# An encoder kernel in fp32r: finishes spread over the scan stage's iterations, and partial sums kept in the matmul banks of the last stages

## The chip, the cores and the metric

The kernel runs on one core of one Trainium2 chip. The time is device microseconds of one launch, and the median over runs is compared. The engines are TensorE (PE in the profile, with its weight loads PEld), VectorE (DVE), ScalarE (ACT), GpSimd (POOL) and SyncE (SP), whose queue issues the DMAs.

## What is computed

One layer of an encoder trunk over a prompt of 1024 tokens and a sample of 512, with 1024 channels. The parts that matter here:

```python
h = _rmsnorm(x, norm_g)
proj = jnp.einsum('bld,de->ble', h, w_in)
(q, f_fw, f_bw, i, z_a, c_B, c_C, c_x, z_b, g_a, g_b) = jnp.split(proj, SPLIT_POINTS, axis=-1)
o_a = _hgrn2_bidir(q, i, f_fw, f_bw, lb_fw, lb_bw, hnorm_g).astype(x.dtype)
p_a = jnp.einsum('ble,ed->bld', o_a * jax.nn.silu(z_a), w_a)
conv = _centred_short_conv(c_C * c_x, conv_w, conv_b)
p_b = jnp.einsum('ble,ed->bld', c_B * conv * jax.nn.silu(z_b), w_b)
merged = jax.nn.sigmoid(g_a) * p_a + jax.nn.sigmoid(g_b) * p_b
return x + jnp.einsum('bld,de->ble', merged, w_o)
```

`_hgrn2_bidir` is a gated linear recurrence in both directions, 8 heads of 128 channels, and a norm per head. A last norm over the channels ends the trunk.

## The kernel before

Every float32 matmul is done as three passes over split operands (`hi`, `lo`; PASSES): ScalarE makes `hi` (L63, "w_h", "s_h"), VectorE the rest (L64, "w_l", "s_l"). Large products of the prompt go by Strassen's scheme in Winograd's form: seven products for eight, with sums of operands before and sums of results after.

Up to 884 us norms and projections run, untouched by the change. Then comes the **scan stage**, to about 1520. Its loop (L670 to L707) has three iterations for each head: the two blocks of the head's prompt group and its sample, m = 0, 1, 2. In an iteration the block loaded before (`prev`) gets its near scores, its keys transposed (L500, copied by ScalarE as kT, L502), its scores (L451, L485) and its contributions (L513: key times value, copied by ScalarE to us, L514); the current block gets its decays (L437, L438 on VectorE, with copies "cat" L435, L436 on ScalarE). Between them stand units: projections of the sample (pp L77), of 24 matmuls each. `outputs` (L537) fills the one bank "o", ScalarE squares and scales it into oz (L541, L545), with a root by GpSimd (rs_o). `finish` (L547 to L553) transposes oz back into a bank "u" (L551), VectorE multiplies it with a gate zg (L552), and it is stored. Banks "u" are three, shared by key transposes, contributions and finishes. In this stage the order on TensorE is the order in which the code is written (order_pe, closed at L989); on the other engines a scheduler sets it, and each engine works its queue in order.

Before the change both blocks of the prompt and the sample's block are finished in iteration m = 2: the prompt's behind the first unit, the sample's ahead of the contributions.

The **last stages** follow from 1591 on: w_b for the prompt, w_b for the sample (from 1667), w_a for the prompt (from 1711), w_a for the sample (from 1787), and the output (from 1830). A prompt stage takes pairs of rows of blocks: `Rows` loads two raws, makes sums S on VectorE (L795 to L800) and splits of 128x1024 (w_h, w_l); `two_blocks` (L820 to L856) then does seven products of 12 matmuls each (L829), every one in a bank "pw" of its own, of five. ScalarE copies the first product, B11, to c11 (L838); VectorE adds T2, T3 and T1 to it in turn (`plus`, L833) and the result is used with an operand more (`use`). The operands of B21 and B22 (`last`, L844) are loaded and split during the first pair, behind its T2; so B21 comes late there. There are 14 pairs: four each in w_b and w_a, six in the output. Here the scheduler sets the order on all engines, TensorE too.

## Time and profile before

| | us |
|---|---|
| runs | 1966.63, 1958.93, 1961.59 (median 1961.59) |
| profiled execution | 1959.61 |
| its span in the trace | 1957.8 |
| TensorE busy | 1918.9 |
| VectorE busy | 1462.7 |
| ScalarE busy | 941.5 |
| mean granted clock of TensorE | 0.993 |

The profiled execution is 1.8 us longer than its span. Busy times are sums over the span; which engine sets the time of a stage is read from what ended each engine's idle time there. A row "PE u L513 <- DVE oz L552" says that TensorE's instruction of line 513, writing a tile u, stood idle until VectorE's instruction of line 552, writing oz, was done.

### The profile page before, as it was taken

Reading aid. Unit: us, or ns where it says so; the run is one execution under the profiler, and the core shown is the slowest. Engines: PE = TensorE matmul, PEld = TensorE weight load, DVE = VectorE, ACT = ScalarE, POOL = GpSimd, SP = SyncE. Lnnn points to the kernel's source line nnn. Section 1 sums busy time; section 2 is a strip of 40 time slices with the busy share of each in tenths; the row PEclk is TensorE's granted clock in tenths of the full one; section 3 lists DMA queues with packets and bytes.
Section 4 is the critical chain, followed back from the end, with each engine's and each line's share of the span. In section 5 each row is a group of like instructions: output and inputs, shape, how many; then the busy total and the mean of one; then the engine's idle time right before and its main releaser. Section 6 shows DMA issues by size and latency. Waiting matters only on the chain.

```text
span 1957.8 us, 38000 instructions
## 1 busy us (share of the span) xinstructions
PE 1918.9 (98%) x14772; PEld 1619.0 (83%) x14772; DVE 1462.7 (75%) x2423; ACT 941.5 (48%) x1946; POOL 144.4 (7%) x220
## 2 busy tenths in 40 slices
PE   8999999999999999999989999999999999999998
PEld 8988888888888888887878888888888888888786
DVE  6558787878787878785776577777773547889996
ACT  6433434434444343434676576676674333434432
POOL 1000000000000000002221122121220000000000
PEclk8999999999999999999999999999999999999999
DMA  7466676676676767668755554554534866879852
GB/s 211 125 212 233 231 232 235 228 238 226 227 245 217 241 230 242 230 211 318 254 184 193 205 196 167 203 198 162 207 132 172 321 232 208 278 236 303 295 175 76
DMA packets 306436, 427.35 MB, mean 218 GB/s; under 512 B 26192, under 2 KB 178000, under 8 KB 306256
## 3 DMA queue, kind: packets, MB, share of 16 engines
q1 hardware_dynamic: 306256, 424.93, 63.9%
q8 instruction: 116, 1.90, 0.4%
q14 instruction: 64, 0.52, 0.1%
HBM read 254.98 MB, written 169.87 MB: 217 GB/s over the span
## 4 chain that ended last, share of the span: by engine, by line
PE 79%; DVE 7%; DMA 4%; issue 4%; ACT 4%; POOL 1%; SPq 0%; DVEq 0%; POOLq 0%; ACTq 0%
PE pp L308 39%; PE pp L77 17%; PE pw L829 9%; PE pp L201 5%; PE pw L77 2%; DVE Q L438 2%; PE o L537 2%; PE u L513 2%; PE sc L451 1%; ACT cat L436 1%; DMA w_raw<-in_w_a 1%; PE pp L70 1%; DVE K L437 1%; POOL rs_o L81 1%; PE u L500 1%
## 5 line engine op out<-in xcount | busy, mean ns | idle before, releaser
L308 PE MATMUL pp<-s_h,w_h 128*128 128x512 f32 x1120 | 435.9, 389 | 1.2 <-ACT w_h L63 1.2
L308 PE MATMUL pp<-s_l,w_h 128*128 128x512 f32 x1120 | 435.7, 389 | 0.0
L308 PE MATMUL pp<-s_h,w_l 128*128 128x512 f32 x1120 | 435.7, 389 | 0.0
L77 PE MATMUL pp<-s_h,w_h 128*128 128x512 f32 x632 | 252.7, 400 | 1.4 <-DMA v<-v_d 0.8
L63 ACT ACTIVATE w_h<-w_raw 128x512 fp32r<-128x512 f32 (+1 forms) x204 | 141.2, 693 | 230.2 <-PE pp L308 151.8
L308 PEld LDWEIGHTS pp<-s_h,w_h 128*128 128x128 f32 x1120 | 210.2, 188 | 45.4 <-ACT w_h L63 1.9
L77 PE MATMUL pp<-s_h,w_l 128*128 128x512 f32 x632 | 247.4, 391 | 0.0
L77 PE MATMUL pp<-s_l,w_h 128*128 128x512 f32 x632 | 246.8, 391 | 0.0
L308 PEld LDWEIGHTS pp<-s_h,w_l 128*128 128x128 f32 x1120 | 210.2, 188 | 43.6
L308 PEld LDWEIGHTS pp<-s_l,w_h 128*128 128x128 f32 x1120 | 210.2, 188 | 43.6
L313 DVE TENSOR_TENSOR tmp<-pp,tmp 128x512 f32<-128x512 f32 x240 | 165.4, 689 | 104.1 <-PE pp L308 103.1
L63 ACT ACTIVATE w_h<-w_S 128x512 fp32r<-128x512 f32 x160 | 99.2, 628 | 186.8 <-PE pp L308 79.6
L64 DVE TENSOR_TENSOR w_l<-w_raw,w_h 128x512 fp32r<-128x512 f32 (+1 forms) x204 | 155.8, 765 | 37.4 <-ACT w_h L63 37.1
L829 PE MATMUL pw<-s_h,w_l 128*128 128x512 f32 x392 | 152.7, 390 | 2.0 <-DVE w_l L64 2.0
L829 PE MATMUL pw<-s_h,w_h 128*128 128x512 f32 x392 | 152.7, 390 | 1.6 <-ACT w_h L63 1.6
L829 PE MATMUL pw<-s_l,w_h 128*128 128x512 f32 x392 | 152.5, 389 | 0.0
L435 ACT COPY cat<-K 128x512 f32<-128x512 f32 x168 | 112.0, 670 | 61.1 <-DVE K L437 23.7
L77 PEld LDWEIGHTS pp<-s_h,w_l 128*128 128x128 f32 x632 | 119.0, 188 | 25.8
L77 PEld LDWEIGHTS pp<-s_h,w_h 128*128 128x128 f32 x632 | 119.5, 189 | 25.0 <-ACT K L132 1.1
L77 PEld LDWEIGHTS pp<-s_l,w_h 128*128 128x128 f32 x632 | 119.6, 189 | 23.4
L436 ACT COPY cat<-Q 128x512 f32<-128x512 f32 x168 | 112.4, 669 | 47.4 <-DVE Q L438 38.3
L438 DVE TENSOR_TENSOR Q<-Q,T 128x512 f32<-128x512 f32 x144 | 111.1, 772 | 27.1 <-ACT cat L436 25.3
(187 smaller groups left out, 3297.9 us busy)
## 6 DMA issues: line engine op xcount, KB each, us to landing
w_raw<-in_w_in SPq DMA_DIRECT2D x80, 512.0 KB, 5.3
ws_d<-w_h SPq DMA_DIRECT2D x160, 256.0 KB, 2.5
ws_d<-w_l SPq DMA_DIRECT2D x160, 256.0 KB, 2.5
w_h<-ws_d SPq DMA_DIRECT2D x79, 512.0 KB, 3.4
w_l<-ws_d SPq DMA_DIRECT2D x79, 512.0 KB, 5.4
fkq_d<-sg SPq DMA_DIRECT2D x48, 256.0 KB, 2.3
v_raw<-in_w_in SPq DMA_DIRECT2D x32, 256.0 KB, 3.5
fkq_d<-sk SPq DMA_DIRECT2D x32, 256.0 KB, 2.3
```

The source lines that it names most:

```text
L63: A.activation(hi, src, AF.Copy)
L64: V.tensor_tensor(lo, src, hi.bitcast(F32), op=ALU.subtract)
L77: T.matmul(out, whl[a][:, k, :], rhs(k, b), start=k == 0 and n == 0, stop=k == KT - 1 and n == 2)
L201: T.matmul(pp, B[f"B{k // 4 + 1}{t + 1}"][a][:, k % 4, c * P:(c + 1) * P], parts[k][b], start=k == 0 and m == 0, stop=k == KT - 1 and m == 2)
L308: T.matmul(bank, hl[x][:, k, :], B[b][y][:, k, :], start=k == 0 and i == 0, stop=k == 3 and i == 2)
L313: V.tensor_tensor(out, p, t, op=ALU.add)
L435: A.copy(ap(cat, 0, [[2 * hs, nb], [hs, 2], [1, hs]]), kall)
L436: A.copy(ap(cat, TB, [[2 * hs, nb], [hs, 2], [1, hs]]), qall)
L438: V.tensor_tensor(qall, qall, ap(t, 1, [[2, nb], [m - 1, 2], [0, hs]]), op=ALU.mult)
L513: T.matmul(p[:, c, :], kT[:, c, :], g.v[:, k.b * CPB + c, :], start=True, stop=True)
L537: T.matmul(p[:, c, :], l, r, start=m == 0, stop=m == len(mms) - 1)
L829: T.matmul(bank, hl[x][:, c:c + P], O[n][y][:, k, :], start=k == 0 and i == 0, stop=k == 3 and i == 2)
```

## The change

`finish` takes one block. Each iteration of the scan finishes one block right behind the key transposes: the sample of the head before last in m = 0, the prompt's two blocks in m = 1 and 2. The outputs of the prompt's second block and of the sample move ahead of the second unit of their iteration, behind the contributions. The gate zgp is loaded right behind the finish.

In the last stages `two_blocks` goes. B11 of a pair is begun while the pair before runs (`begun`); T2, T3 and T4 then add into the same bank, and ScalarE copies the bank between them (c11, u2, u3). B22 adds into T1's bank. VectorE adds a copy to a bank once in each use, and the adds `plus` are gone. `last()` comes directly behind the first product of a stage.

```diff
--- before.py
+++ after.py
@@ -544,8 +544,8 @@
                 for c in range(CPB):
                     A.activation(oz[:, c, :], p[:, c, :], AF.Copy, scale=r[:, c:c + 1])
 
-        def finish(g):
-            for k in g.done:
+        def finish(g, b):
+            for k in g.done[b:b + 1]:
                 p = bank("u", 3)
                 for c in range(CPB):
                     T.transpose(p[:, c, :], k.oz[:, c, :], ident)
@@ -677,29 +677,24 @@
             if prev:
                 near_scores(prev)
                 transpose_keys(prev)
+            if i > 3:
+                finish(*((sample[h - 2].g, 0) if m == 0 else (groups[h - 1], m - 1)))
             if m == 0 and h:
                 outputs(groups[h - 1], 0)
+            if m == 2:
+                groups[h].zg = gtile("zgp", [2 * TB])
+                load(groups[h].zg, zg_d[h])
             if cur:
                 decays(cur)
                 if cur.b == 0:
                     values(cur.g)
             unit()
-            if m == 2 and h:
-                finish(groups[h - 1])
             if prev:
                 scores(prev)
-            if m == 2:
-                if h:
-                    finish(sample[h - 1].g)
-                groups[h].zg = gtile("zgp", [2 * TB])
-                load(groups[h].zg, zg_d[h])
-            if prev:
                 contributions(prev)
+            if m < 2 and h:
+                outputs(*((sample[h - 1].g, 0) if m else (groups[h - 1], 1)))
             unit()
-            if m == 0 and h:
-                outputs(groups[h - 1], 1)
-            if m == 1 and h:
-                outputs(sample[h - 1].g, 0)
             if m != 1:
                 unit()
             if prev and len(prev.g.done) == len(prev.g.tbs):
@@ -707,8 +702,9 @@
             prev = cur
         outputs(sample[NH - 1].g, 0)
         unit()
-        finish(groups[NH - 1])
-        finish(sample[NH - 1].g)
+        for b in range(2):
+            finish(groups[NH - 1], b)
+        finish(sample[NH - 1].g, 0)
         left.close()
         right.close()
 
@@ -814,46 +810,56 @@
         def products(O, last, r, srcs, use):
 
 
-
+            def prod(hl, half, n, bank=None):
+                start = bank is None
+                if start:
+                    bank = ps.tile([P, TB], F32, name="pw", bufs=5)
+                for k in range(4):
+                    for i, (a, b) in enumerate(PASSES):
+                        c = half * TB + k * P
+                        T.matmul(bank, hl[a][:, c:c + P], O[n][b][:, k, :],
+                                 start=start and k == 0 and i == 0, stop=k == 3 and i == 2, skip_group_check=True)
+                return bank
+
+            def copied(bank):
+                c = wk.tile([P, TB], F32, name="c", bufs=6)
+                A.copy(c, bank)
+                return c
+
+            def begun(r):
+                r.x = prod(r.f, 0, "B11")
+                r.c11 = copied(r.x)
+
+            begun(r)
+            last()
             i = 0
             while r.raws:
-                r = two_blocks(O, r, partial(use, i), None if i else last, partial(srcs, i + 1))
+                if i:
+                    r.sums(0)
+                    r.sums(1)
+                ahead = Rows(srcs(i + 1))
+                if i == 0:
+                    y = prod(r.s12, 0, "T1")
+                prod(r.s12, 1, "T2", r.x)
+                u2 = copied(r.x)
+                if i == 0:
+                    ahead.first()
+                    begun(ahead)
+                else:
+                    y = prod(r.s12, 0, "T1")
+                prod(r.s34, 0, "T3", r.x)
+                u3 = copied(r.x)
+                use(i, 0, 0, prod(r.f, 1, "B21"), r.c11)
+                use(i, 1, 1, y, u3)
+                prod(r.last, 0, "T4", r.x)
+                use(i, 1, 0, r.x, None)
+                if i and ahead.raws:
+                    ahead.first()
+                    begun(ahead)
+                prod(r.s34, 1, "B22", y)
+                use(i, 0, 1, y, u2)
+                r = ahead
                 i += 1
-
-        def two_blocks(O, r, use, last, later):
-            def prod(hl, half, n):
-                bank = ps.tile([P, TB], F32, name="pw", bufs=5)
-                for k in range(4):
-                    for i, (x, y) in enumerate(PASSES):
-                        c = half * TB + k * P
-                        T.matmul(bank, hl[x][:, c:c + P], O[n][y][:, k, :], start=k == 0 and i == 0, stop=k == 3 and i == 2)
-                return bank
-
-            def plus(out, p, t):
-                V.tensor_tensor(out, p, t, op=ALU.add)
-
-            c11, c12, c21 = (wk.tile([P, TB], F32, name="c", bufs=6) for _ in range(3))
-            if not last:
-                r.first()
-            A.copy(c11, prod(r.f, 0, "B11"))
-            if not last:
-                use(0, 0, c11, prod(r.f, 1, "B21"))
-                r.sums(0)
-            plus(c12, prod(r.s12, 1, "T2"), c11)
-            if last:
-                last()
-            else:
-                r.sums(1)
-            ahead = Rows(later())
-            plus(c21, prod(r.s34, 0, "T3"), c12)
-            p5 = prod(r.s12, 0, "T1")
-            plus(c12, p5, c12)
-            use(1, 1, c21, p5)
-            use(1, 0, c21, prod(r.last, 0, "T4"))
-            if last:
-                use(0, 0, c11, prod(r.f, 1, "B21"))
-            use(0, 1, c12, prod(r.s34, 1, "B22"))
-            return ahead
 
         def plain(whl, act):
             pp = ps.tile([P, TB], F32, name="pw", bufs=5)
@@ -893,10 +899,11 @@
                         pb[j] = io.tile([P, 2, TB], F32, name="io")
                         load(pb[j].rearrange("p a b -> p (a b)"), pb_x[0][j])
 
-            def use(i, m, t, c, more):
+            def use(i, m, t, u, more):
                 m += 2 * i
-                u = wk.tile([P, TB], F32, name="sum", bufs=2)
-                V.tensor_tensor(u, more, c, op=ALU.add)
+                if more is not None:
+                    V.tensor_tensor(more, u, more, op=ALU.add)
+                    u = more
                 finish_block(m, t, s[m], u)
 
             r = prepared(srcs)
@@ -917,8 +924,8 @@
             pb = {}
 
             def block(m, t, s, u):
-                V.tensor_tensor(u, u, s[:, t, :], op=ALU.mult)
-                V.tensor_tensor(s[:, t, :], u, pb[m][:, t, :], op=ALU.add)
+                V.tensor_tensor(s[:, t, :], u, s[:, t, :], op=ALU.mult)
+                V.tensor_tensor(s[:, t, :], s[:, t, :], pb[m][:, t, :], op=ALU.add)
                 left_of[m] = left_of.get(m, 0) + 1
                 if left_of[m] == 2:
                     store(m_x[0][m], s.rearrange("p a b -> p (a b)"))
@@ -951,7 +958,8 @@
                 n = 2 * i + m
                 x = xt[n][:, h, :]
                 V.tensor_tensor(x, c, x, op=ALU.add)
-                V.tensor_tensor(x, more, x, op=ALU.add)
+                if more is not None:
+                    V.tensor_tensor(x, more, x, op=ALU.add)
                 A.activation(ps.tile([P, TB], F32, name="junk"), x, AF.Square, scale=D ** -0.5, accum_out=ss[n][:, h:h + 1])
                 halves[n] = halves.get(n, 0) + 1
                 if halves[n] == 2:
```

How the instructions move, at three places. The first is the iteration m = 2 that ends the third head, on TensorE: a unit (L77, tile pp_12368 before, pp_12384 after) with what stands around it. Before:

```order
L500 MATMUL u_12296<-ident_60,K_11532 128x128 x3
L500 MATMUL u_12302<-ident_60,K_11532 128x128 x4
L77 MATMUL pp_12368<-s0_h_8404,w_h_11873 128x512
...
L77 MATMUL pp_12368<-s1_h_8406,w_l_11874 128x512
L551 MATMUL u_12396<-ident_60,oz_11631 128x128 x4
L551 MATMUL u_12403<-ident_60,oz_11860 128x128 x4
L451 MATMUL sc_12410<-cat_12027 32x32 x16
...
L485 MATMUL sc_12470<-cat_12042 64x64 x8
L551 MATMUL u_12481<-ident_60,oz_12207 128x128 x4
L513 MATMUL u_12490<-v8_11697,kT_12300 128x128 x3
L513 MATMUL u_12495<-v8_11697,kT_12307 128x128 x4
L77 MATMUL pp_12505<-s0_h_8404,w_h_12047 128x512
```

and after:

```order
L500 MATMUL u_12303<-ident_60,K_11525 128x128 x3
L500 MATMUL u_12309<-ident_60,K_11525 128x128 x4
L551 MATMUL u_12316<-ident_60,oz_11827 128x128 x4
L77 MATMUL pp_12384<-s0_h_8404,w_h_11873 128x512
...
L77 MATMUL pp_12384<-s1_h_8406,w_l_11874 128x512
L451 MATMUL sc_12412<-cat_12034 32x32 x16
...
L485 MATMUL sc_12472<-cat_12049 64x64 x8
L513 MATMUL u_12483<-v8_11697,kT_12307 128x128 x3
L513 MATMUL u_12488<-v8_11697,kT_12314 128x128 x4
L77 MATMUL pp_12498<-s0_h_8404,w_h_12054 128x512
```

The transposes of oz (L551) stood between the unit and the contributions, three banks of them; now one stands ahead of the unit, behind the key transposes.

The same iteration on VectorE, where Q, K are the decays of the next block. Before:

```order
L438 TENSOR_TENSOR Q_12309<-Q_12309,T2_12313 128x128x2x2
L437 TENSOR_TENSOR K_11845<-K_11845,T8_12317 128x32x2x8
L438 TENSOR_TENSOR Q_12309<-Q_12309,T4_12315 128x64x2x4
L438 TENSOR_TENSOR Q_12309<-Q_12309,T8_12317 128x32x2x8
L552 TENSOR_TENSOR oz_11631<-u_12396,zgp_11442 128x512
L552 TENSOR_TENSOR oz_11860<-u_12403,zgp_11442 128x512
L437 TENSOR_TENSOR K_11845<-K_11845,T16_12319 128x16x2x16
```

and after:

```order
L437 TENSOR_TENSOR K_11870<-K_11870,T2_12329 128x128x2x2
...
L438 TENSOR_TENSOR Q_12325<-Q_12325,T2_12329 128x128x2x2
...
L552 TENSOR_TENSOR oz_11827<-u_12316,zgp_11277 128x512
L464 COPY_PREDICATED near_12298<-mk_973,sc_12233 128x128
L437 TENSOR_TENSOR K_11870<-K_11870,T4_12331 128x64x2x4
```

The multiplies L552 came behind the decays of levels 2, 4 and 8; the one now left in this iteration stands ahead of those of level 4.

The second place is the first pair of the output on ScalarE: io are rows of w_o, s5 and s6 the operands of B21 and B22, w_raw and S the rows of the products, c the copies of banks. Before:

```order
L63 ACTIVATE w_h_19681<-S_19678 128x1024
L838 COPY c_19695<-pw_19698 128x512
L63 ACTIVATE s5_h_19726<-io_19730 128x512
L63 ACTIVATE s6_h_19728<-io_19730 128x512
L63 ACTIVATE w_h_19687<-S_19678 128x1024
...
L63 ACTIVATE s5_h_19726<-io_19736 128x512
...
L63 ACTIVATE s5_h_19726<-io_19748 128x512
L63 ACTIVATE s6_h_19728<-io_19748 128x512
L63 ACTIVATE w_h_19864<-w_raw_19754 128x1024
```

and after (c_19693 copies the bank behind T2):

```order
L63 ACTIVATE w_h_19607<-S_19598 128x1024
...
L826 COPY c_19628<-pw_19615 128x512
L63 ACTIVATE s5_h_19630<-io_19634 128x512
L63 ACTIVATE s6_h_19632<-io_19634 128x512
L63 ACTIVATE s5_h_19630<-io_19640 128x512
...
L63 ACTIVATE s5_h_19630<-io_19652 128x512
L63 ACTIVATE s6_h_19632<-io_19652 128x512
L826 COPY c_19693<-pw_19615 128x512
L63 ACTIVATE w_h_19695<-w_raw_19658 128x1024
...
L826 COPY c_19726<-pw_19615 128x512
```

All eight splits of s5 and s6 now stand ahead of a copy for which T3 waits; before, T3 had a bank of its own.

The third is the first pair of w_a on ScalarE (s2 and s4 are the operands of B21 and B22). Before:

```order
L63 ACTIVATE w_h_18826<-w_raw_18726 128x1024
L63 ACTIVATE s4_h_18700<-io_18702 128x512
L63 ACTIVATE s2_h_18698<-io_18708 128x512
L838 COPY c_18667<-pw_18670 128x512
L63 ACTIVATE s4_h_18700<-io_18708 128x512
...
L63 ACTIVATE s4_h_18700<-io_18720 128x512
```

and after, where c_18640 is the copy of B11 for which T2 waits:

```order
L63 ACTIVATE s2_h_18642<-io_18646 128x512
L63 ACTIVATE w_h_18709<-w_raw_18670 128x1024
L63 ACTIVATE s4_h_18644<-io_18646 128x512
L63 ACTIVATE s2_h_18642<-io_18652 128x512
L63 ACTIVATE s4_h_18644<-io_18652 128x512
L826 COPY c_18640<-pw_18627 128x512
L63 ACTIVATE s2_h_18642<-io_18658 128x512
```

The copy stands behind both splits of the second row, io_18652, where one stood ahead of it.

## Rows read from the trace of the kernel before

**Rows 1.** the page's first part: busy us, share of the span and instructions of each engine

```profile
PE 1918.9 (98%) x14772; PEld 1619.0 (83%) x14772; DVE 1462.7 (75%) x2423; ACT 941.5 (48%) x1946; POOL 144.4 (7%) x220
```

**Rows 2.** TensorE's waits: instruction <- what it waited for: us in total, times, longest

```profile
PE u L513 <- DVE oz L552: 13.9, 7, 2.4
...
PE u L513 <- ACT us L514: 2.5, 1, 2.5
PE pw L829 <- DVE w_l L64: 2.0, 3, 0.8
PE pw L829 <- ACT w_h L63: 1.6, 2, 1.0
```

**Rows 3.** timeline of TensorE around one head's finishes: start us, us, instruction [idle before <- releaser]

```profile
1161.29 1.06 PE L451 MATMUL sc<-cat 128*32 128x32 f32 x96
...
1162.89 1.83 PE L513 MATMUL u<-v,kT 128*128 128x128 f32 x14
1164.48 0.48 PE L77 MATMUL pp<-s_h,w_h 128*128 128x512 f32 x1
...
1170.03 0.38 PE L537 MATMUL o<-v,pt 128*128 128x128 f32 x2
...
1171.37 0.61 PE L537 MATMUL o<-us,Q 128*128 128x128 f32 x4
...
1182.49 0.66 PE L551 MATMUL u<-ident,oz 128*128 128x128 f32 x4
1185.42 3.19 PE L513 MATMUL u<-v,kT 128*128 128x128 f32 x14 [2.27 <-DVE oz L552]
```

**Rows 4.** timeline of VectorE at the same place

```profile
1184.07 0.69 DVE L438 TENSOR_TENSOR Q<-Q,T 128x512 f32<-128x512 f32 x1 [0.69 <-ACT cat L436]
1184.68 1.28 DVE L552 TENSOR_TENSOR oz<-u,zgp 128x512 f32<-128x512 f32 x2
```

**Rows 5.** windows: stretch, us, busy us (x instructions) of each engine, PEclk, DMA share, GB/s

```profile
1024.00:1028.00 4.00, 2.67 (x10) 2.54 (x11) 4.00 (x8) 3.58 (x7) 2.49 (x4) 0.56 0.00 0
1028.00:1032.00 4.00, 4.00 (x12) 3.13 (x11) 3.66 (x12) 2.14 (x9) 0.00 (x0) 0.59 0.80 217
1400.00:1404.00 4.00, 4.00 (x18) 3.83 (x19) 3.65 (x8) 2.84 (x8) 0.49 (x2) 0.58 0.84 251
```

**Rows 6.** timeline of ScalarE behind the outputs of a sample

```profile
1175.77 1.14 ACT L545 ACTIVATE oz<-o,rs_o 128x128 f32<-128x128 f32 x4 [1.56 <-POOL rs_o L81]
...
1176.94 0.99 ACT L502 COPY kT<-u 128x384 f32<-128x384 f32 x2
```

**Rows 7.** groups by line from 1591 on: shapes xcount | busy us, mean ns | idle before

```profile
L833 DVE TENSOR_TENSOR c<-pw,c 128x512 f32<-128x512 f32 x42 | 28.9, 688 | 13.0 <-PE pw L829 12.7
L63 ACT ACTIVATE w_h<-S 128x1024 fp32r<-128x1024 f32 x26 | 27.3, 1059 | 63.5 <-DVE S L800 37.3 <-PE pw L829 17.9 <-DVE S L796 4.7
...
L838 ACT COPY c<-pw 128x512 f32<-128x512 f32 x14 | 8.1, 577 | 9.1 <-PE pw L829 9.1
```

**Rows 8.** windows of two stretches of the last stages

```profile
1711.00:1787.00 76.00, 76.00 (x337) 62.95 (x336) 66.77 (x100) 25.89 (x35) 0.00 (x0) 1.00 0.78 257
1830.00:1850.00 20.00, 17.20 (x72) 12.99 (x71) 19.77 (x30) 10.19 (x15) 0.00 (x0) 1.00 0.95 320
```

**Rows 9.** timeline of ScalarE in the first blocks of w_b, w_a and output

```profile
1598.17 2.44 ACT L63 ACTIVATE s_h<-io 128x512 fp32r<-128x512 f32 x4 [3.79 <-DMA io<-cz_p]
...
1602.74 2.18 ACT L63 ACTIVATE s_h<-io 128x512 fp32r<-128x512 f32 x4
...
1719.53 0.63 ACT L63 ACTIVATE s_h<-io 128x512 fp32r<-128x512 f32 x1 [3.12 <-DMA io<-oz_p]
...
1842.20 2.43 ACT L63 ACTIVATE s_h<-io 128x512 fp32r<-128x512 f32 x4 [1.72 <-DMA io<-in_w_o]
```

**Rows 10.** timeline of TensorE where the output begins

```profile
1831.03 0.50 PE L829 MATMUL pw<-s_h,w_h 128*128 128x512 f32 x1 [0.63 <-ACT w_h L63]
```

**Rows 11.** timeline of VectorE behind the last product

```profile
1950.84 0.68 DVE L954 TENSOR_TENSOR io<-pw,io 128x512 f32<-128x512 f32 x1
```

## The prediction, made before the changed kernel ran

> **What bounds the kernel now.** The page comes first: TensorE is busy 98% of the span, VectorE 75%, ScalarE 48% [rows 1]. A change that removes no TensorE product can therefore gain only TensorE's idle time and the time in which its clock is low; taking adds off VectorE is worth nothing by itself. So I read next the table of who waited for whom on TensorE [rows 2]. The dearest line is L513, the contributions of the scan stage, waiting for VectorE's multiply L552: 13.9 us in 7 waits, once in each head from the second on. It is followed once by a wait of 2.5 us of the same line for a ScalarE copy. In the last stages, which the other half of the change rewrites, the products L829 wait only 2.0 and 1.6 us, all in the first block of the output.
>
> The timeline shows why L513 waits [rows 3]. The four transposes of the sample's block (L551) run at 1182.49 for 0.66 us; the contributions start at 1185.42 only, after 2.27 us of nothing. They take a bank "u", and all three are held by transposes that VectorE has not yet read. VectorE reaches its two L552 at 1184.68, since they stand behind the decay products L438 in its queue, and the contributions start when the first of them ends [rows 4]. VectorE is not full; its order is what costs.
>
> The wait has a second price. The windows show the granted clock at 0.56 and 0.59 over 1024 to 1032, and 0.58 over 1400 to 1404, behind three of these waits [rows 5]; the clock has two levels, 1.2 and 2.4 GHz. The 14 contributions at 1185.42 took 3.19 us, those at 1162.89 took 1.83 [rows 3].
>
> **The finishes, part by part.** The change does one finish of four transposes in each iteration, directly behind transpose_keys, instead of one of eight and one of four in every third. Between it and the contributions now stands a whole unit, 1164.48 to 1170.03 or 5.55 us [rows 3], and the scores. VectorE had its two L552 done 3.5 us after the start of the late transposes (1182.49 to 1184.68 + 1.28) [rows 3, 4]; with 5.55 us and more in between the wait disappears. Nothing else holds the contributions at that place: the key copies kT that they read were made at 1176.94, over 7 us ahead of them [rows 6]. Removed: 13.9 us, and the 2.5 us that follow the first of them [rows 2].
>
> The clock: in 1024 to 1028 TensorE was busy 2.67 us at 0.56, which loses 1.2; 4 us at 0.59 lose 1.6; 4 us at 0.58 lose 1.7 [rows 5]; the contributions at 1185.42 lose 3.19 - 1.83 = 1.4 [rows 3]. That is 5.9 us. Other gaps of this list did not lower the clock, so it goes only if no gap of this length is left; I take all of it. Sum of this part: -(13.9 + 2.5 + 5.9) = -22.3, with -14 as the poor end (half the clock back, and a wait of 0.8 us in each head).
>
> What is moved with it: outputs(groups, 1) and outputs(sample) come one unit earlier. They share the one bank "o", which is free when ScalarE's scaled copies L545 end: outputs end at 1171.98, L545 at 1176.91, so 4.9 us [rows 3, 6]. The new distance from outputs 0 to outputs 1 is one unit (5.55) plus scores and contributions (1161.29 to 1164.48, 3.2), 8.7 us in all; 3.8 are to spare. Cost zero. The load of zgp moves up in SyncE's queue: it waits for an L552 that now comes a unit earlier as well, and the weights behind it belong to units three places on. Cost zero. The total of transposes, multiplies and stores is unchanged.
>
> **The last stages, part by part.** Per pair of blocks three L833 adds and one add of the use go, 4 x 14 = 56 VectorE instructions of 0.688 us, 38.5 us [rows 7]. VectorE is busy 66.8 of 76 us in the w_a stage and 19.8 of 20 us where the output begins [rows 8], but TensorE, which sets the end, waits there only as in rows 2. I cost this at nothing. ScalarE gains two copies of 0.577 us for each pair [rows 7], and those stand on TensorE's path: T2, T3 and T4 add into the bank that holds B11, so T2 may not begin before B11 is copied, nor T3 before T2's sum is, nor T4 before T3's is. In the later blocks another product stands in between each time. A product is 2.72 us: the w_a stage has 28 of them in its 76 us [rows 8]. A copy of 0.58 has 2.1 us to spare, which is two weight splits of 1.06 [rows 7]. There I find no more than that queued ahead: nothing.
>
> The three first blocks are different, since last() now comes at once: the splits of the last two operands stand ahead of the copies in ScalarE's queue, and those splits wait for loads.
> - w_b: T3 is the fifth product, due 10.9 us after the stage's start at 1591, at 1601.9. Four operand splits begin at 1598.17 and end at 1600.6 [rows 9]; a weight split and the copy end at 1602.2 to 1602.8. I take 0.5 us; 0 to 2.2, if the four splits that begin at 1602.74 came first.
> - w_a: T2 is the third product, due 5.4 us after the stage's start at 1711, at 1716.4. The copy of B11 stands behind two rows of splits; the second row's split began at 1719.53, held by its load, and the copy could end at about 1721.2 [rows 9]. That is 4.8 us, if the load comes as late. The load waits for a slot that VectorE's earlier work frees, and VectorE has less of it, so it may cost nothing. Middle: 2.5.
> - output: three products from 1831.03, where the first of its gaps ends [rows 10], are 8.2 us, and some 2.2 of the gaps of rows 2 lie among them: T2 ends at about 1841.3. T2's copy stands behind all eight splits, the last four of which ran from 1842.20 to 1844.63, held by their load [rows 9]; with 0.57 for the copy T3 begins at 1845.2, 4 us late. The next block's B11, now begun here, may wait 0.5 for its weights. Less crowded queues take back some of this and of the 3.6 us of rows 2: net +2.7, between 0 and +4.7.
> At the very end two adds follow the last product where one did, 0.68 us at 1950.84 [rows 11]: +0.65. Sum of this part: 0.5 + 2.5 + 2.7 + 0.65 = +6.4, from about 0 to +13.
>
> A rule that speaks against this half: the Trainium skill, PSUM — Partial Sum Buffer, section "PSUM bank collisions raise a hardware error", says that two engines may not touch one bank at the same time, so software must keep TensorE out while ScalarE reads. By it, and with nothing between product and copy, 14 x 3 copies would lie on the path: 42 x 0.58 = +24 us. The order of the products puts one between; no run so far shows such a wait.
>
> **The sum.** 1959.61 (the profiled execution) - 22.3 + 6.4 = 1943.7. That execution stands 2.0 below the median of the runs, so 1945.7 for the median.
>
> **Rivals.**
> 1. All copies come in time: only the tail is added, -22.3 + 0.65 makes 1939.9. For it speaks the emptier VectorE; against it that the loads, not VectorE, ended last for ScalarE in rows 9.
> 2. The gain of the finishes is mostly given back by ScalarE's queue in the three first blocks: 2.2 + 4.8 + 4.7 + 0.65, and the clock falls behind two such gaps of 4 and 5 us as it did behind the 2.4 us ones, at 1.7 each: +16. 1961.6 - 22.3 + 16 = 1955.4, no change that can be measured.
> 3. Bank "o": if ScalarE's copies of the scores, which now run between the squares and L545, make 4.9 us into over 8.7, outputs 1 wait. At 1.5 us in each of 8 heads this is 12 us: 1957.7. The margin of 3.8 us speaks against it.
> 4. Slower: the copies of the sums are late in every pair, not in the first alone. The point is 2.72 us after a product's end. With three weight splits ahead of a copy it comes 3 x 1.06 + 0.58 - 2.72 = 1.0 us late; 42 of these are +44: 1989. From 0.62 us for each copy the kernel is slower by over 0.5%. For it speaks that a split on ScalarE can itself wait for VectorE's sums; against it that ScalarE is busy less than half the time and that the next sums are begun a block ahead.
>
> **How the numbers follow.** 0.5% of 1961.6, or 9.8 us, is about what a measurement of this kernel can tell from no change. Forecast 0.45, rival 1 0.17, rival 2 0.20, rival 3 0.07, rival 4 0.11. The forecast's own bounds are -22.3 + 0 and -14 + 8, 1939 to 1956, nearly all below 1951.8. Faster: nearly all of the forecast, all of rival 1, a fifth of rival 2, less than half of rival 3: 0.67. Slower is rival 4, 0.11. The rest, 0.22, is the same. The range leaves out rival 4 and the worst of rivals 2 and 3 above and the best of rival 1 below: 1938 to 1957.
>
> **What the changed profile would show.** Right: no L513 waiting for L552 or for the us copy in the table of waits, and a granted clock of 1.00 over the scan stage; the waits of the products for copies c, 2 to 5 us each, in the first blocks alone, and a VectorE total lower by some 38 us. Wrong: L513 or the transposes waiting for another releaser in every head (then my reading of the "u" banks fails); o waiting for L545 (rival 3); waits for c in most blocks (rival 4); or no wait for c at all (rival 1).

## The result, and the profile after

The changed kernel takes 1940.72 us (median of 4 runs, 1938.58 to 1942.72) against 1960.26 for the kernel before in the same runs (1958.39 to 1966.63): a ratio of 0.9894, 95% interval 0.9869 to 0.992. It is faster by some 20 us; 1945.7 was predicted, 1938 to 1957 the range.

The profiled execution took 1942.72 us, its span is 1940.9. Its page and its table of TensorE's waits, in the columns of [rows 1] and [rows 2]:

```profile
PE 1913.4 (99%) x14772; PEld 1613.8 (83%) x14772; DVE 1428.3 (74%) x2367; ACT 957.3 (49%) x1974; POOL 151.9 (8%) x220
```

```profile
PE pw L820 <- ACT c L826: 6.1, 2, 3.9
...
PE u L500 <- DVE K L437: 1.4, 1, 1.4
...
PE pp L77 <- ACT K L132: 1.2, 1, 1.2
...
PE pw L820 <- DVE w_l L64: 1.0, 1, 1.0
...
PE pw L820 <- ACT w_h L63: 0.4, 1, 0.4
```

The row of L513, 13.9 us in [rows 2], is gone, and that of the us copies with it. New is the first row: the products of the last stages (now L820) wait 6.1 us for ScalarE's copies c, in two waits. VectorE has 34.4 us less to do (some 38 were predicted), ScalarE 15.8 more.

The stages as the starts of their first matmuls divide them, in us; "output" ends with the last matmul, "tail" with the span:

| kernel | scan | w_b | w_b sample | w_a | w_a sample | output | tail |
|---|---|---|---|---|---|---|---|
| before | 708.2 | 76.2 | 43.5 | 76.2 | 43.5 | 119.3 | 8.1 |
| after | 683.1 | 76.4 | 43.5 | 82.0 | 43.5 | 120.5 | 8.8 |
| difference | -25.1 | +0.2 | 0 | +5.9 | 0 | +1.2 | +0.7 |

("scan" here reaches from 883 to the first product of w_b; idle time ahead of a stage is counted to the stage.) The sum is -17.1, and 0.2 were lost before 883: the spans differ by 16.9. The medians differ by 2.6 us more because the profiled execution of the changed kernel is the slowest of its four, 2.0 us above their median, and that of the kernel before stands 0.65 below its own.

Where the scan's 25.1 us went can be added up from the trace, from each matmul's start to the next one's. TensorE's idle time falls from 20.1 to 3.4 us, or 16.7. The contributions L513, the outputs L537 and the units L77 together take some 6 us less, by the clock. And the transposes of the finishes L551 take 9.3 us for 12.6, the key transposes L500 0.9 more: 2.4 us that nobody had forecast, or 0.1 us for each finish that follows the key transposes directly. The timeline of TensorE in one head's iteration m = 2 has the place that answers to [rows 3]:

```profile
1164.34 0.98 PE L500 MATMUL u<-ident,K 128*128 128x128 f32 x7
1165.16 0.60 PE L551 MATMUL u<-ident,oz 128*128 128x128 f32 x4
...
1171.18 1.06 PE L451 MATMUL sc<-cat 128*32 128x32 f32 x96
1172.17 0.69 PE L485 MATMUL sc<-cat 128*64 128x64 f32 x16
1172.78 1.83 PE L513 MATMUL u<-v,kT 128*128 128x128 f32 x14
```

The four transposes run at 1165.16, a whole unit lies between, and the contributions follow the scores at 1172.78 without a gap, in 1.83 us for the 3.19 of [rows 3]. The window of the scan stage shows the granted clock at 1.00 (its columns are those of [rows 5]):

```profile
884.00:1520.00 636.00, 632.56 (x8755) 538.62 (x8754) 452.12 (x820) 421.79 (x1075) 137.10 (x192) 1.00 0.60 211
```

### The profile page after: what moved, and what is told of

Same layout as the page of the kernel before. It is cut to its first block, busy times and chain, and to the rows that moved or that the text cites. A ratio compares the mean times of both kernels' runs of the same rounds, so it can differ in the third digit from the quotient of the medians.

```text
span 1940.9 us, 37940 instructions
## 1 busy us (share of the span) xinstructions
PE 1913.4 (99%) x14772; PEld 1613.8 (83%) x14772; DVE 1428.3 (74%) x2367; ACT 957.3 (49%) x1974; POOL 151.9 (8%) x220
## 4 chain that ended last, share of the span: by engine, by line
PE 90%; DMA 5%; DVE 2%; ACT 1%; issue 1%; SPq 0%; DVEq 0%; POOLq 0%; POOL 0%; ACTq 0%
PE pp L308 39%; PE pp L77 21%; PE pw L820 12%; PE pp L201 5%; PE o L537 3%; PE sc L451 3%; PE u L513 2%; PE pp L70 2%; PE u L500 1%; PE sc L485 1%; DMA io<-oz_p 1%; DMA w_raw<-in_w_a 1%; DMA io<-in_w_o 1%; DVE s_l L64 1%; PE tp L163 1%
## 5 line engine op out<-in xcount | busy, mean ns | idle before, releaser
L77 PE MATMUL pp<-s_h,w_h 128*128 128x512 f32 x632 | 250.6, 396 | 1.2 <-ACT K L132 1.2
L77 PE MATMUL pp<-s_h,w_l 128*128 128x512 f32 x632 | 246.4, 390 | 0.0
L77 PE MATMUL pp<-s_l,w_h 128*128 128x512 f32 x632 | 246.2, 390 | 0.0
L820 PE MATMUL pw<-s_h,w_h 128*128 128x512 f32 x392 | 154.0, 393 | 6.5 <-ACT c L826 6.1
L820 PE MATMUL pw<-s_h,w_l 128*128 128x512 f32 x392 | 153.8, 393 | 1.0 <-DVE w_l L64 1.0
L820 PE MATMUL pw<-s_l,w_h 128*128 128x512 f32 x392 | 154.0, 393 | 0.0
L77 PEld LDWEIGHTS pp<-s_h,w_l 128*128 128x128 f32 x632 | 118.6, 188 | 25.3
L77 PEld LDWEIGHTS pp<-s_h,w_h 128*128 128x128 f32 x632 | 118.8, 188 | 24.7 <-ACT K L132 1.6
L77 PEld LDWEIGHTS pp<-s_l,w_h 128*128 128x128 f32 x632 | 118.9, 188 | 23.3
L436 ACT COPY cat<-Q 128x512 f32<-128x512 f32 x168 | 112.0, 667 | 30.1 <-DVE Q L438 23.3
L437 DVE TENSOR_TENSOR K<-K,T 128x512 f32<-128x512 f32 x144 | 107.6, 747 | 23.0 <-ACT cat L435 21.1
```

The costliest lines, as they stand in the source:

```text
L77: T.matmul(out, whl[a][:, k, :], rhs(k, b), start=k == 0 and n == 0, stop=k == KT - 1 and n == 2)
L436: A.copy(ap(cat, TB, [[2 * hs, nb], [hs, 2], [1, hs]]), qall)
L437: V.tensor_tensor(kall, kall, ap(t, m + 1, [[2, nb], [-m - 1, 2], [0, hs]]), op=ALU.mult)
L820: T.matmul(bank, hl[a][:, c:c + P], O[n][b][:, k, :], start=start and k == 0 and i == 0, stop=k == 3 and i == 2, skip_group_check=True)
```

## The experiments

### Each half by itself

The kernel before, with the scan's lines of the change alone (finish, outputs, the load of zgp), and with the lines of `products` alone.

> Only the scan stage's half of the change (one finish in each iteration behind the key transposes, outputs one unit earlier); the last stages as before. Theory: the two halves are independent, and the trace of the changed kernel has this half at 25 us (w_b begins at 1565.98 for 1590.87): about 1935 us against 1960, below the changed kernel by 5 to 8. Rival one: this half gives only the 22.3 of the forecast and the emptier VectorE of the last stages gave the rest: 1938. Rival two: the last stages gain too, so that this half alone stands above the changed kernel: over 1941.

> Only the last stages' half; the scan stage as before. Theory: this half costs 8 us, two gaps for the copies c in the first pairs of w_a and of the output, the clock behind each, and 0.7 in the tail, against 3.6 us of gaps that it partly removes: 1968 us against 1960. Rival: without the other half the loads and the queues stand otherwise and it costs nothing or gains: 1957 to 1961.

Measured on one chip: the scan's half 1933.31 us, ratio 0.9852 (0.9833 to 0.9871); the last stages' half 1966.7 us, ratio 1.0012 (1.0 to 1.0024), against 1964.08 before. So the scan's half alone is better than the whole change. The last stages' half costs 2.6 us by itself (0 to 5 by the interval); with the scan mended the two ratios, 0.9852 and 0.9894, put it at 8 us, and the second measurement below (0.9866) at 5. That it costs more there is not shown: the intervals are too wide to tell 2.6 us from 5 or 8. The theory had the sign of both right; of the 8 us that it gave to the second half 2.6 were measured with the scan as it was. The stages say where the half costs and gains, though not how much in the median: the profiled execution of the last stages' half, 1958.36 us, was the fastest of twelve. In it w_a takes 81.2 us, 5 more than before, but the output 116.3, 3 less. With the scan's half alone (an execution of 1937.42 us, 4 above its median) the output takes 123.6, 4.3 more than before; its table of waits has the reason in its first row:

```profile
PE pw L825 <- ACT w_h L63: 4.6, 1, 4.6
```

One wait of 4.6 us for the weights of the output's first product, and the granted clock is at its lower level for 6.8 us around it. The timeline of SyncE's queue and of ScalarE's shows what held them:

```profile
1799.68 0.38 SPq L933 DMA_DIRECT2D m_s<-io  x1
1800.10 1.43 SPq L764 DMA_DIRECT2D w_raw<-m_p  x2
...
1807.40 1.06 ACT L63 ACTIVATE w_h<-w_raw 128x1024 fp32r<-128x1024 f32 x1 [1.97 <-DMA w_raw<-m_p]
```

The output's rows (w_raw from m_p) were issued at 1800.10 only, behind a store of m_s in the same queue, and ScalarE sat idle for 1.97 us until they landed. In the changed kernel they were issued 33.7 us after the w_a sample stage began, here 39.9: VectorE, with fewer adds, finishes what that store waits for sooner. A later experiment takes that up.

### The copies and the loads ahead of them

The changed kernel with `last()` moved behind the copy of T2's sum and B21 behind T4, in the first pair of each stage:

```diff
             begun(r)
-            last()
...
                 u2 = copied(r.x)
                 if i == 0:
+                    last()
...
-                use(i, 0, 0, prod(r.f, 1, "B21"), r.c11)
+                if i:
+                    use(i, 0, 0, prod(r.f, 1, "B21"), r.c11)
...
                 use(i, 1, 0, r.x, None)
+                if i == 0:
+                    use(i, 0, 0, prod(r.f, 1, "B21"), r.c11)
```

> The changed kernel, with last() called behind the copy of T2's sum instead of behind the first product, and B21 behind T4, in the first pair of each stage alone. Theory: the copies were late because the splits of the last two operands, held by their loads, stood ahead of them: the gaps of 3.9 and 2.2 us and the clock behind them (3.4) go, and what stays is at most 1.5 us for sums that now follow each other closely: 1931 to 1934 us. Rival: ScalarE is held at that place by other loads (the next pair's rows) all the same, the gaps get another releaser and the time stays at 1939 to 1942.

Measured: 1949.7 us, ratio 0.9926 (0.9912 to 0.994), some 6 us slower than the changed kernel by the ratios; its span is 6.8 us longer. Both expectations fail in their numbers. Its waits:

```profile
PE pw L820 <- ACT s_h L63: 6.0, 2, 5.2
PE pw L820 <- ACT w_h L63: 3.2, 3, 1.6
PE pw L820 <- DVE w_l L64: 1.5, 2, 1.1
...
PE pw L820 <- ACT c L826: 1.2, 3, 0.7
```

The waits for c shrink from 6.1 us to 1.2, so the copies were late by what stood ahead of them, as the theory has it. But the splits of the last two operands now come later still, and in w_a a product waits 5.2 us for them (s_h; by the order of the code it is B21); w_a grows to 88.4. The wait did not go, it changed its name. The timeline of the changed kernel shows that the loads set both; ScalarE in the first pair of w_a and of the output, with TensorE behind it (they answer to [rows 9] and [rows 10]):

```profile
1693.68 1.15 ACT L63 ACTIVATE s_h<-io 128x512 fp32r<-128x512 f32 x2 [1.93 <-DMA io<-oz_p]
1694.74 0.57 ACT L826 COPY c<-pw 128x512 f32<-128x512 f32 x1
...
1695.36 0.50 PE L820 MATMUL pw<-s_h,w_h 128*128 128x512 f32 x1 [3.88 <-ACT c L826]
```

```profile
1822.29 1.15 ACT L63 ACTIVATE s_h<-io 128x512 fp32r<-128x512 f32 x2 [1.43 <-DMA io<-in_w_o]
1823.35 0.57 ACT L826 COPY c<-pw 128x512 f32<-128x512 f32 x1
...
1823.96 0.50 PE L820 MATMUL pw<-s_h,w_h 128*128 128x512 f32 x1 [2.21 <-ACT c L826]
```

Each time a pair of splits begins after ScalarE sat idle for a load of the operand (1.93 and 1.43 us), the copy of 0.57 us follows it, and the product that adds into the copied bank starts when the copy ends.

So the first pair was given back its old form, a bank for each product and the sums on VectorE, with the next pair's B11 begun behind T4:

```diff
-            begun(r)
-            last()
-            i = 0
-            while r.raws:
...
+            A.copy(c11, prod(r.f, 0, "B11"))
+            plus(c12, prod(r.s12, 1, "T2"), c11)
+            last()
+            ahead = Rows(srcs(1))
+            plus(c21, prod(r.s34, 0, "T3"), c12)
...
+            added(1, 0, c21, prod(r.last, 0, "T4"))
+            ahead.first()
+            begun(ahead)
+            added(0, 0, c11, prod(r.f, 1, "B21"))
+            added(0, 1, c12, prod(r.s34, 1, "B22"))
...
+            i = 1
+            while r.raws:
```

(`plus` and `added` are the adds of the kernel before; the loop below runs the later pairs unchanged.)

> The changed kernel, with the first pair of each prompt stage done as before (a bank for each product, sums on VectorE, last() behind T2, B21 behind T4), its B11 of the next pair begun behind T4; the later pairs stay as changed. Theory: the harm of the last stages' half is all in the first pairs; the 5.9 us of the w_a stage and the 2.2 us gap of the output with its clock go, and the gain at the output's start stays: 1931 to 1934 us. Rival: as with last() moved alone, the loads of the last operands come late all the same and the wait only gets another name: 1940 or more.

Measured: 1932.19 us, ratio 0.9847 (0.9833 to 0.9862), as the theory said. w_a takes 76.2 us again, the output 115.3, and the table of waits has one row left for these products:

```profile
PE pw L820 <- ACT w_h L63: 0.5, 1, 0.5
```

The harm was in the first pairs alone; in the later pairs the sums in the banks cost TensorE nothing. Both this kernel and the scan's half were then run once more on one chip.

> The scan stage's half alone once more, on the same chip as the next kernel: 1932 to 1937 us. If the last stages' half has any worth left when its first pairs are done as before, this one is the slower of the two by 2 to 8 us (its output stage took 123.6 us against 115.3).

> The changed kernel with the first pair of each prompt stage done as before, once more, on the same chip as the scan's half alone: 1929 to 1934 us. By the stages of its trace it should be 8 us below the scan's half alone; the rival is that the two are equal, the gap at the output's start coming and going with the order of SyncE's queue.

Measured: the scan's half 1936.17 us, ratio 0.9866 (0.9853 to 0.988); with the last stages' half mended 1931.14, ratio 0.9844 (0.983 to 0.9857). That is 5 us, less than the 8 of the single traces, and the intervals just touch: this time the scan's half had its first wait in the output at 0.5 us, not at 4.6. So that wait differs between executions of one kernel. The mended kernel is the fastest of this study, 9 to 10 us below the changed one; over the scan's half it gains 1 us by the first ratios of the two (0.9847, 0.9852) and 4 by the second (0.9844, 0.9866).

### VectorE's adds given back

```diff
                 use(i, 0, 1, y, u2)
+                for _ in range(4):
+                    V.tensor_tensor(wk.tile([P, TB], F32, name="more", bufs=2), u3, u3, op=ALU.add)
```

> The changed kernel with four more VectorE adds (128x512, into a tile that nobody reads) behind each pair of the prompt stages, as many as the change took away. Theory: with the scan's half alone TensorE waited 4.6 us for the output's first rows, which stood in SyncE's queue behind a store that waits for VectorE; the adds taken away are what brought them in time: the gap comes back, 3 to 5 us with the clock behind it: 1945 to 1949 us. Rival: VectorE's adds are off the path and cost nothing; the gap there came from another order of the queue: 1939 to 1942 us.

Measured: 1941.92 us, ratio 0.9899 (0.9884 to 0.9914), no different from the changed kernel's 0.9894. The time goes to the rival, the mechanism to the theory:

```profile
PE pw L820 <- ACT c L826: 4.6, 2, 3.6
...
PE pw L820 <- ACT w_h L63: 2.8, 1, 2.8
```

TensorE now waits 2.8 us for the output's first weights; in the changed kernel the first product waited for nothing (its 0.4 us for w_h stand ahead of the second). But the copies are waited for less (4.6 us for 6.1), in the output since TensorE now comes to them later, and the sum is nearly the same: output 121.7 us against 120.5. So the adds do move the start of the output, and they are worth nothing while a later wait takes it back.

All the traces agree on the start. The first load of the output's rows is issued 36.6 to 40.8 us after the start of the w_a sample stage in the six traces with the old number of adds (the two of the scan's half at 39.9 and 36.6), and 32.2 to 34.2 us after it in seven with fewer. The one exception is the kernel with `last()` moved, 38.2, whose w_a stage ran 12 us longer.

### What held up the scan stage

The one finish of each iteration, placed behind the unit instead of behind the key transposes:

```diff
-            if i > 3:
-                finish(*((sample[h - 2].g, 0) if m == 0 else (groups[h - 1], m - 1)))
...
             unit()
+            if i > 3:
+                finish(*((sample[h - 2].g, 0) if m == 0 else (groups[h - 1], m - 1)))
             if prev:
                 scores(prev)
```

> The changed kernel with its one finish in each iteration placed behind the unit, just ahead of the scores, and not behind the key transposes. Theory as in the prediction (what counts is the unit between finish and contributions): L513 waits for L552 again, some 1 to 2 us in most of the 24 iterations: 1965 to 1985 us. Rival (what counts is that one finish leaves two of the three u banks to the contributions, wherever it stands): no wait, only the transposes, which cost TensorE about 0.14 us more each time when they don't follow the key transposes: 1942 to 1945 us.

Measured: 1941.69 us, ratio 0.9889 (0.9873 to 0.9906). No wait came back, so the unit in between was not what the gain rested on. The rival, the number of u banks, was put to the test by finishing both prompt blocks there, and the sample at m = 0 as in the change:

```diff
-            if i > 3:
-                finish(*((sample[h - 2].g, 0) if m == 0 else (groups[h - 1], m - 1)))
+            if i > 3 and m == 0:
+                finish(sample[h - 2].g, 0)
...
-            if m == 2:
-                groups[h].zg = gtile("zgp", [2 * TB])
-                load(groups[h].zg, zg_d[h])
...
             unit()
+            if m == 2:
+                if h:
+                    finish(groups[h - 1], 0)
+                    finish(groups[h - 1], 1)
+                groups[h].zg = gtile("zgp", [2 * TB])
+                load(groups[h].zg, zg_d[h])
```

> The changed kernel with both prompt blocks finished in m = 2 behind the unit, just ahead of the scores, as before, and only the sample's finish elsewhere (m = 0, behind the key transposes). Theory (one finish leaves two of the three u banks to the contributions; two leave one): the second half of the contributions in m = 2 waits for the first L552, 0.5 to 2 us in each of 8 heads, with the clock behind some: 1946 to 1960 us. Rival (it was the third bank, the sample's transposes, or the place, that made the wait): no wait, 1939 to 1944 us.

Measured: 1940.14 us, ratio 0.9891 (0.9874 to 0.9907); again no row of L513 in the table of waits. The bank alone does not explain the wait either. The timelines of TensorE and VectorE show what differs from [rows 3] and [rows 4]:

```profile
1169.13 1.03 PE L551 MATMUL u<-ident,oz 128*128 128x128 f32 x8
...
1171.70 2.07 PE L513 MATMUL u<-v,kT 128*128 128x128 f32 x14
...
1170.98 0.98 DVE L438 TENSOR_TENSOR Q<-Q,T 128x512 f32<-128x512 f32 x1
1171.88 1.27 DVE L552 TENSOR_TENSOR oz<-u,zgp 128x512 f32<-128x512 f32 x2
```

The transposes start at 1169.13 and VectorE is at its first L552 2.75 us later; the second half of the contributions waits for it so shortly that 14 of them take 2.07 us for 1.83. In the kernel before the same pair of finishes started here:

```profile
1179.93 1.03 PE L551 MATMUL u<-ident,oz 128*128 128x128 f32 x8
```

and L552 at 1184.68 [rows 4], 4.75 us later. VectorE is earlier by two microseconds. What these two kernels have in common is the place of the outputs, and the sample's finish, which is gone from m = 2. The outputs were put back first:

```diff
-            if m < 2 and h:
-                outputs(*((sample[h - 1].g, 0) if m else (groups[h - 1], 1)))
             unit()
+            if m < 2 and h:
+                outputs(*((sample[h - 1].g, 0) if m else (groups[h - 1], 1)))
```

> The changed kernel with the outputs of the prompt's second block and of the sample behind the second unit of their iteration, as before. Theory: the move neither gains nor costs, bank o having 3.8 us to spare: 1939 to 1943 us. Rival: the earlier outputs are part of the gain (their oz is ready sooner for the next finish): L551 or L513 waits again in every head, 1945 us or more.

Measured: 1942.34 us, ratio 0.9901 (0.9886 to 0.9916), and no wait of L513; the scan takes 684.2 us. With one finish in each iteration the place of the outputs does not matter. Then each of the two was done alone on the kernel before: the outputs moved and all three finishes left in m = 2, or the sample's finish moved and the rest left.

```diff
+            if m == 0 and h:
+                outputs(groups[h - 1], 1)
+            if m == 1 and h:
+                outputs(sample[h - 1].g, 0)
             unit()
-            if m == 0 and h:
-                outputs(groups[h - 1], 1)
-            if m == 1 and h:
-                outputs(sample[h - 1].g, 0)
```

> The kernel before, with only the outputs of the prompt's second block and of the sample moved ahead of the second unit of their iteration; all three finishes stay in m = 2. Theory (ScalarE's work for the sample's outputs, at 1172 to 1177, held up the decays' copies, and with them VectorE's decays ahead of L552): the 13.9 us of L513 waiting for L552 mostly go, 1938 to 1948 us. Rival (it is the third u bank, taken by the sample's transposes just ahead of the contributions): the waits stay, 1957 to 1965 us, with 5 to 14 us in that row.

```diff
+            if i > 3 and m == 0:
+                finish(sample[h - 2].g)
             if m == 0 and h:
                 outputs(groups[h - 1], 0)
...
-                if h:
-                    finish(sample[h - 1].g)
```

> The kernel before, with only the sample's finish moved, to m = 0 behind the key transposes; the two prompt blocks are finished in m = 2 behind the unit, and the outputs stay where they were. Theory (ScalarE's output work made L552 late, whatever the banks): the wait stays, in the second half of the contributions now, so some 0.8 us shorter in each head: 7 to 10 us in that row, 1950 to 1960 us. Rival (the third u bank): the first half of the contributions finds a free bank and the wait goes: 1938 to 1946 us.

Measured: outputs alone 1936.49 us, ratio 0.9868 (0.9855 to 0.9882), no different from the scan's half (0.9866 on the same chip); the scan takes 684.1 us for 682.7 there, the difference being the transposes (L551 12.0 us for 9.3, L500 17.5 for 18.7), and L513 waits for nothing. It is a little below what the theory gave. The sample's finish alone: 1955.99 us, ratio 0.9966 (0.9954 to 0.9978), in the theory's range, but with a row that was sized wrongly, since the second half of the contributions waits as long as the whole did (14.2 us, not 7 to 10):

```profile
PE u L513 <- DVE oz L552: 14.2, 7, 2.6
```

(It still gains 7 us in the median and 3 us of the scan by the traces: the 2.5 us wait for the us copy is gone, and L551 takes 11.0 us for 12.6.)

The theory on ScalarE holds in sign in both. Its chain can be read in the two traces. ScalarE and VectorE in the kernel with only the sample's finish moved:

```profile
1169.10 1.21 DVE L417 SCALAR_TENSOR_TENSOR Q<-q,F 128x1024 f32<-128x1024 f32 x1
...
1172.47 1.14 ACT L545 ACTIVATE oz<-o,rs_o 128x128 f32<-128x128 f32 x4 [2.16 <-POOL rs_o L81]
...
1174.47 0.92 ACT L436 COPY cat<-Q 128x512 f32<-128x512 f32 x1
...
1175.42 1.16 DVE L438 TENSOR_TENSOR Q<-Q,F 128x512 f32<-128x512 f32 x1 [0.63 <-ACT cat L436]
...
1181.37 1.28 DVE L552 TENSOR_TENSOR oz<-u,zgp 128x512 f32<-128x512 f32 x2
...
1182.11 1.16 PE L513 MATMUL u<-v,kT 128*128 128x128 f32 x8 [2.58 <-DVE oz L552]
```

and in the kernel with only the outputs moved:

```profile
1163.59 1.14 ACT L545 ACTIVATE oz<-o,rs_o 128x128 f32<-128x128 f32 x4 [0.61 <-POOL rs_o L81]
1164.60 0.87 ACT L436 COPY cat<-Q 128x512 f32<-128x512 f32 x1
...
1165.51 1.17 DVE L438 TENSOR_TENSOR Q<-Q,F 128x512 f32<-128x512 f32 x1 [1.32 <-ACT cat L436]
...
1173.03 1.27 DVE L552 TENSOR_TENSOR oz<-u,zgp 128x512 f32<-128x512 f32 x2
...
1173.14 0.66 PE L551 MATMUL u<-ident,oz 128*128 128x128 f32 x4
1173.76 1.83 PE L513 MATMUL u<-v,kT 128*128 128x128 f32 x14
```

With the outputs behind the second unit, ScalarE's scaled copies L545 of the sample end at 1173.6, behind an idle time of 2.16 us for the root rs_o, and the copy cat of Q that the decays need (L436) stands behind them: 1174.47. VectorE can begin the decays of Q at 1175.42 and gets to L552 at 1181.37, too late. With the outputs a unit earlier the same copy is made at 1164.60, the decays of Q begin at 1165.51, and L552 comes at 1173.03, in time: the contributions follow the last transposes at once, though three u banks are full. The two clocks differ: the second kernel is 5.5 us ahead by then (its key transposes L500 start at 1164.25, those of the first at 1169.73). Counted from these transposes the copy comes 0.4 us behind them for 4.7, and L552 8.8 us for 11.6. So L552 is 2.9 us earlier, a little more than the wait of 2.58 that is gone.

The outputs do one thing more: they read the Q of the sample before, whose buffer the new Q takes. That was not what held it up here: L417 had written Q by 1170.31, 4.2 us ahead of its copy. No run changes ScalarE's order and nothing else, so this chain is read from the traces; what the experiments show is that, with all finishes left in m = 2, the outputs' place alone decides whether L513 waits.

## Why the prediction was right, and where its reasons were not

**The bound.** That the kernel waits on TensorE for L513, and that the gain is those waits with their clock, was right: the idle time of the scan fell by 16.7 us, and -(13.9 + 2.5) was the term.

**The clock.** 5.9 us were taken, some 6 found, in the two profiled executions. How much the clock costs differs between executions of the kernel before: of 17 on one chip the fastest took 1958.24 us at a mean granted clock of 0.993, the slowest 1967.95 at 0.990.

**The finishes.** The step "with 5.55 us and more in between the wait disappears" gave the right number and half a reason. The unit in between is not needed: with the finish behind the unit there was no wait. And the step "Cost zero" for the outputs failed: this move was priced for what it could harm, bank o, and not for what it frees. (Its margin is misread too: L537 runs to 1172.4, not 1171.98, so 4.2 us were to spare and not 3.8.) On the kernel before it alone brings the gain, but for the 1.4 us of the transposes. Either one is enough: one finish in each iteration with the outputs left, or the outputs earlier with the finishes left. The prediction read in [rows 4] that L552 stood behind the decays, and did not ask what the decays were late for; the row itself names it, an idle time of VectorE that a copy cat L436 ended, and [rows 6] show what ScalarE did ahead of it. What is not settled is which of the two moved outputs does it; the sample's stands next to the place.

**What was missing.** The 2.4 us by which transposes that follow transposes are shorter. They make most of the difference between the 25.1 of the scan and the 22.3 that were forecast. Placed apart (the two kernels with finishes behind the unit) L551 takes 12.3 and 11.0 us in place of 9.3, and L500 17.5 in place of 18.6.

**The last stages.** The mechanism was right, ScalarE's copies behind splits that wait for loads, in the first pairs alone, and the steady pairs clean. Sizes: w_b 0.5 predicted, 0.2 found; w_a 2.5 (bound 4.8), found 5.9, of which 3.9 are the gap and most of the rest the clock behind it (3.4 us at the lower level, which costs 1.7), which this term had left out; output 2.7 (0 to 4.7), found 1.2, gaps of 3.6 us in all as before, one of 2.2 us for a copy among them, but 3.4 us at the lower clock behind that one; tail 0.65, found 0.7. Sum 6.4 predicted, 8.0 found. The middle value for w_a was too kind: that VectorE had less to do hardly brought the load forward. It was issued 4.4 us after the stage's start in both kernels, and landed 7.8 us after it for 9.0.

**The sum.** By the traces -15.9 was forecast and -16.9 found, which is closer than the terms were: the scan gave 2.8 us more and the last stages cost 1.6 more, and the two misses half cancel. That is luck. Most of the 5 us between the 1945.7 of the forecast and the median of 1940.72 is in the step from one execution to the median: it added 2.0 us, and the profiled execution of the changed kernel stands 2.0 above its median.

**VectorE's adds.** "I cost this at nothing" held in the time of the kernel with the adds given back. By the stages it was not quite nothing: they decide when the output's first rows are loaded, no waiting of its first product against 2.8 us, and this can count where nothing later takes it back, as in the kernel with the old first pairs.

**The rivals.** Rival 1 (all copies in time, 1939.9) did not come true, since two copies were late; with the first pairs done as before none is, and the time is 1931 to 1932 us. Rival 2 came true for w_a alone. Rival 3, bank o, showed nowhere: no o waits in any table. Rival 4 showed in no later pair. The rule of the Trainium skill weighed there (PSUM — Partial Sum Buffer, section "PSUM bank collisions raise a hardware error") agrees with the trace as far as it goes: each of the two waits for c ends when the copy does. What happens when the two engines do meet in a bank no run shows. And the copy costs only where it is late; with a product in between its 0.57 us cost nothing.

## What to carry to other kernels

When a wait names an instruction that is late in its engine's queue, follow the queue back to what made that one late, over the other engines; the cheapest cure may be a step that seems to have nothing to do with the wait. A sum kept in the matmul's bank saves adds on one engine and puts copies of another on TensorE's path: at the start of a stage, where the copying engine waits for loads, give each product a bank of its own, and keep the scheme for the steady pairs. And measure the two halves of a change apart: here one gains 27 to 31 us by itself and the other costs 0 to 5, which the 20 of the whole don't tell.

## What the runs showed of the hardware

The length of a gap does not tell by itself whether the clock falls. In the kernel with only the sample's finish moved a gap of 2.12 us left the clock where it was, and one of 1.52 us did not, as the same eight contributions behind each show:

```profile
1022.36 1.16 PE L513 MATMUL u<-v,kT 128*128 128x128 f32 x8 [2.12 <-DVE oz L552]
...
1109.09 1.88 PE L513 MATMUL u<-v,kT 128*128 128x128 f32 x8 [1.52 <-DVE oz L552]
```

They took 1.16 us behind the longer gap and 1.88 behind the shorter. The windows show the granted clock at 1.00 and 0.67 (columns as in [rows 5]):

```profile
1024.00:1028.00 4.00, 4.00 (x19) 3.26 (x19) 4.00 (x7) 3.95 (x9) 2.52 (x3) 1.00 0.02 4
1108.00:1112.00 4.00, 2.91 (x11) 2.67 (x12) 4.00 (x9) 2.89 (x7) 0.69 (x2) 0.67 0.57 168
```

What made the difference is open.

And transposes of one size took TensorE less time in a row than apart: the 96 of the finishes took 9.3 us behind the key transposes and 12.3 between a unit and the scores, from each start to the next instruction's. The key transposes took 18.6 us in the first kernel and 17.5 in the second, so both together are shorter by 1.9 us.
